# One more pair of K tiles through seven products in a feed-forward output projection

## The chip, the cores and the metric

The kernel runs on one NeuronCore of a Trainium2 chip. The metric is the device time of one execution in microseconds; the kernel before has a median of 1604.06 us over three runs. A change of some 0.2% of that, 3.2 us, is about what a measurement can tell from none.

## What is computed

The reference is one layer of an encoder over two sequences of 512 tokens with a model width of 1024: three branches (a state-space scan, a differential attention, a cross attention to a memory), their gated merge, and a gated feed-forward part with a hidden width of 2816. Only its last lines are touched here:

```
x = x + merged @ p['w_out'][l]
xn2 = _rmsnorm(x, p['norm_ffn'][l])
gate, up = jnp.split(xn2 @ p['w_ffn_in'][l], 2, axis=-1)
return x + (jax.nn.silu(gate) * up) @ p['w_ffn_out'][l]
```

After that comes a last `_rmsnorm` over the model width. All of it is float32. The product by `w_ffn_out` has 2816 = 22 x 128 rows to sum over, 22 **K tiles**, 8 output tiles of 128 model columns, and 1024 tokens (two sequences of 512).

## The kernel before, in words

**Precision by three matmuls.** Every operand is split into a rounded high part and the remainder (`split`, line 131: a cast on ACT at line 134 or 137 and a subtraction on DVE at line 135 or 138), and a product is three matmuls: high by high, high by low, low by high. One matmul has 128 rows of weights and up to 512 columns; all of them are issued at line 66. A matmul's result lies in one of eight PSUM banks, six under the tag `mm` and two under `tr` (line 928); a bank can be written anew when its reader is through.

**Seven products in place of eight.** A block of two by two tiles (two output tiles m and m+4, two K tiles 2p and 2p+1, the two sequences) can be multiplied with seven products of sums of tiles in place of eight, so 21 matmuls and not 24. Such a pair of K tiles needs, on the side of the activations, three sums on DVE and one on POOL (`quad_sums`, line 966), seven operands split into high and low (`quad_split`, line 983: four casts, four subtractions), and rooms for them (`quad_room`, line 977: four rooms in all, so pair i takes the room of pair i-4, and of i-4 only after its last matmul). A pair is made by `act_pair` (line 1117: two loads from DRAM, where the gated stage left its result `aD`, and the sums) and `pair_in` (line 1183). On the side of the weights it needs, for each of the four pairs of output tiles, a **piece**: seven sums of weight tiles with their splits. There are `NPAIR` x 4 pieces, and `NPREP` (line 40) says how each is got. The first 16 are wholly made beforehand, beside the attention, and written to DRAM; the next ones, up to the second number, have four of their seven made beforehand, in the gated stage (`prepare`, line 459, one half-piece per iteration by `half_piece`, line 491), and the other three made on the spot; the rest are wholly made on the spot (`weights7`, line 1213, with four additions on POOL in `raw_sums`, line 451).

**The gated stage.** The 22 tiles of the hidden width are made in a loop, each by seven products of four K blocks, 84 matmuls; the half-pieces are prepared in iterations 1 and on. Its pools are closed and the next stage's opened three iterations before the end.

**The visits.** The output projection goes in twelve visits (`VISITS`, line 35: a row m of output tiles and a range of pairs). A visit runs through its pairs, seven products each, adding up in seven banks; then seven sums on DVE (`quadrants`, line 1104, written at 1101) put the products together into four tiles, and four additions on POOL (line 1274) add them to the output y. For visit v the loop at line 1246 names where pairs are made: pair 4 within visit 3, others after visits 0, 1, 3, 4, 6 and 7. Weights for piece n+2 are loaded and for n+1 split while piece n is multiplied; their rooms rotate through six slots (`w_room`, line 1207).

**The plain part.** The K tiles that no pair takes (`nb` = 4 with nine pairs) are done by three matmuls each, at the end: first for the first sequence at 512 columns, then for each half of the second at 256. For every output tile DVE adds the bank to y (line 1345), ACT squares it, POOL adds the squares up (`sum_sq`, line 175). Then a root, a reciprocal and a transpose on PE (`factor`, line 195) give the norm, and eight scalings (line 1327 on DVE, some on POOL at line 1322) and the stores to the output follow (`final`, line 1313). The weights of the plain part are loaded in the last two visits (`keep`, line 1193) into rooms of a pair that has been used up, and split when the plain part begins; its four activations are split after visit 8 (line 1285 on).

**What sets the order.** From the last iteration of the gated stage to the end of the visits PE keeps the order in which the program is written; in the plain part and on the other engines a scheduler puts instructions in the order in which, by its own estimate, they can start, and in the order of the program where several can. Each engine then works through its list strictly in order. All transfers are issued from SP.

Of the kernel before, what the change touches and what calls it, by code (L numbers as in the profile page):

```python
# [19 lines left out]
P = 128  # L20
L = 512
# [7 lines left out]
KFF = FF // P  # L29
# [2 lines left out]
G = 32  # L32


VISITS = ((0, 0, 2), (1, 0, 3), (2, 0, 3), (3, 0, 4), (0, 2, 5), (1, 3, 6), (2, 3, 6), (3, 4, 7), (0, 5, 9), (1, 6, 9),
          (2, 6, 9), (3, 7, 9))
NPAIR = 9


NPREP = (16, 28)  # L40

NG = (7, 6, 3)

# [29 lines left out]
def encoder(ctx: ExitStack, tc: tile.TileContext, a, out):  # L73
    nc = tc.nc
# [31 lines left out]
    def slot(tag, shape=(P, NT), dt=F32, name="sl"):  # L106
        return pools[tag].tile(list(shape), dt, tag=tag, name=name)

    def bank(tag="mm"):
        return pools[tag].tile([P, 512], F32, tag=tag, name="bk" + tag)  # L110

    def aux():
        return bank("tr")
# [17 lines left out]
    def split(hi, lo, src, scale=None):  # L131

        if scale is None:
            h = S.copy(hi, src)  # L134
            l_ = V.tensor_tensor(out=lo, in0=src, in1=hi.bitcast(F32), op=ALU.subtract)  # L135
        else:
            h = S.activation(out=hi, in_=src, func=AF.Copy, scale=scale)
            l_ = V.scalar_tensor_tensor(out=lo, in0=src, scalar=scale, in1=hi.bitcast(F32), op0=ALU.mult, op1=ALU.subtract)
        return h, l_
# [47 lines left out]
    def rstd(acc, n, nt=4):  # L187


        ss = aux()  # L190
        for t in range(nt):
            PE.matmul(ss[:, t : t + 1], acc[:, t * P : (t + 1) * P], onec[:, 0:1], start=(t == 0), stop=(t == nt - 1))
        return factor(ss, n, nt)

    def factor(ss, n, nt=4, bias=epsc):

        rs = rp.tile([P, 4], F32, tag="rs", name="rs", bufs=4)
        S.activation(out=rs[:, :nt], in_=ss[:, :nt], func=AF.Sqrt, scale=1.0 / n, bias=bias)
        V.reciprocal(rs[:, :nt], rs[:, :nt])
        bc = aux()  # L200
        for t in range(nt):
            PE.transpose(bc[:, t * P : (t + 1) * P], rs[:, t : t + 1].broadcast_to([P, P]), ident)
        return rs, bc
# [89 lines left out]
    def queued():  # L293

        return tc.issue_after(last_w.ins)
# [54 lines left out]
    with yielding(last_s):  # L350
        x_norm(0, norm[0], range(5, 8))
        _, bc = factor(ss1, DM)
# [78 lines left out]
    for nm in ("c", "s"):  # L431
        r_ = rpp.tile([P, L], F32, tag=f"r{nm}", name=f"r{nm}")
# [4 lines left out]

    pieces = [(m, p) for m, lo_, hi_ in VISITS for p in range(lo_, hi_)]
    pieces = [(m, p, 7 if i < NPREP[0] else 4 if i < NPREP[1] else 0) for i, (m, p) in enumerate(pieces)]
    wD = {(m, p): drp.tile([P, n, 2, P], F32, name=f"wD{m}_{p}") for m, p, n in pieces if n}  # L440
# [18 lines left out]
    def prepare(es_, todo_):  # L459
        pq = es_.enter_context(tc.tile_pool(name="pq", bufs=1, side="right", reuse_waits="tile"))  # L460
        raws = []

        def load():
            if len(raws) < len(todo_):
                raws.append(pq.tile([P, 4, P], F32, tag="raw", name="raw", bufs=4))
                with queued():
                    raw_in(raws[-1], *todo_[len(raws) - 1][:2])

        def part(n_, j, w_):
            m, p, _ = todo_[n_]  # L470
            k = w_.shape[1]
            hl = pq.tile([P, k, 2, P], F32R, tag=f"hl{k}", name="hl", bufs=k // 2)
            split(hl[:, :, 0], hl[:, :, 1], w_, scale=0.5)
            nc.sync.dma_start(wD[m, p][:, j : j + k], hl.bitcast(F32))

        for _ in range(3):
            load()
        yield
        for n_, (m, p, k) in enumerate(todo_):
            load()  # L480
            if k == 7:
                part(n_, 4, raws[n_][:, 1:4])
            if k == 7 or n_ == 0:
                raw_sums(raws[n_])
                yield
            part(n_, 0, raws[n_])
            if n_ + 1 < len(todo_) and todo_[n_ + 1][2] == 4:
                raw_sums(raws[n_ + 1])
            yield
# [99 lines left out]
    pes = ExitStack()  # L589
    prep = prepare(pes, pieces[: NPREP[0]])  # L590
    next(prep)
# [87 lines left out]
    ld = lp.tile([P, 2], F32, tag="ld", name="ld", bufs=1)  # L679
# [11 lines left out]
    for i in range(-AHEAD, len(steps) + 1):  # L691
# [24 lines left out]
        if i > 0 and steps[i - 1][2] == 3:  # L716
            h, s, _ = steps[i - 1]
# [185 lines left out]
    n = len(steps)  # L903
# [73 lines left out]
    def quad_room(i):  # L977
        j = i // 2 % 2
        return slot(f"th{j}", [P, 7, L], F32R, "th"), slot(f"tl{j}", [P, 7, L], F32R, "tl")
# [3 lines left out]
    def quad_split(i, xa_, xb_, t_):  # L983

        nonlocal last_q
        th, tl = quad_room(i)
        split(th[:, 0], tl[:, 0], xa_[:, 0:L])
        split(th[:, 1:3].rearrange("p a n -> p (a n)"), tl[:, 1:3].rearrange("p a n -> p (a n)"), xb_)
        split(th[:, 3:5], tl[:, 3:5], t_[:, 0:2])
        last_q = split(th[:, 5:7], tl[:, 5:7], t_[:, 2:4])  # L990
        return th, tl
# [66 lines left out]
    aD = [drp.tile([P, NT], F32, name=f"aD{i}") for i in range(KFF)]  # L1058
# [75 lines left out]
    for i in range(KFF):  # L1134
        w = nxt_w or all7(i)
        nxt_w = None
        if i == 1:
            prep = prepare(pes, pieces[NPREP[0] : NPREP[1]])
            next(prep)
# [11 lines left out]
        if i == 0:  # L1151
            for s in range(NS):
                _, bc = rstd(accs[s], DM)
                S.copy(accs[s], bc)
        gf0, gf1, up0, up1 = quadrants(ps, p0)
        ac = ap2.tile([P, NT], F32, tag="ac", name="ac")
# [26 lines left out]
    def pair_in():  # L1183
        pairs.append(quad_split(len(pairs), *act_pair(len(pairs))))


    nb = KFF - 2 * NPAIR
    kept, lasts = [], []

    def last_rows(m):  # L1190
        return a["w_fo"][m, :, 2 * NPAIR * P :]

    def keep(n):
        if not kept:
            lasts.extend(quad_room(NPAIR + 1))
        for _ in range(n):
            i = len(kept)
            if i % 2 == 0:
                lasts[2:] = [slot("ld", [P, 2, L], name="fw")]
            k0, k1, raw = lasts  # L1200
            with queued():
                nc.sync.dma_start(raw[:, i % 2], last_rows(i + 1))
            kept.append((k0[:, i], k1[:, i], raw[:, i % 2]))

    n_w, last_7 = 0, None

# [38 lines left out]
    n_p = 0  # L1245
    for v, (m, lo_, hi_) in enumerate(VISITS):
        ps = [bank() for _ in range(6)] + [aux()]
        for p in range(lo_, hi_):
            if n_p + 2 < len(pieces):
                next(coming[n_p + 2])  # L1250
            for g in coming[n_p + 1 : n_p + 2]:
                for _ in g:
                    pass
            th, tl = pairs[p]
            w = made[n_p]
            n_p += 1
            if v < 4 and p == 1:
                with queued():
                    for t in (m, m + 4):
                        nc.sync.dma_start(y[t], x1D[t])  # L1260
            for p_, (nm, o) in zip(ps, SEVEN):
                wh, wl = w[nm]
                PE.matmul(p_, wh, th[:, o], start=(p == lo_), stop=False)
                PE.matmul(p_, wh, tl[:, o], start=False, stop=False)
                PE.matmul(p_, wl, th[:, o], start=False, stop=(p == hi_ - 1))
            if v == 3 and p == 0:
                pair_in()
            if (v, p) in ((10, 7), (10, 8), (11, 7), (11, 8)):
                keep(1 if v == 10 and p == 7 else 2)
        ps = iter(ps)  # L1270
        c11, c12, c21, c22 = quadrants(ps, next(ps), ("nsq", "nsq"))
        for c_, t, s in ((c11, 0, 0), (c22, 4, 1), (c21, 4, 0), (c12, 0, 1)):
            yv = y[m + t][:, s * L : (s + 1) * L]
            PO.tensor_tensor(out=yv, in0=yv, in1=c_, op=ALU.add)
        if v == 0:
            with tc.issue_after(last_sum.ins):
                pairs.append(quad_split(2, *nxt))
        elif v == 1:
            with queued(), tc.issue_after(last_sum.ins):
                pair_in()  # L1280
        for _ in range({3: 1, 4: 1, 6: 1, 7: 1}.get(v, 0)):
            pair_in()
        if v == 8:

            r0, r1 = quad_room(NPAIR)
            r2 = slot("ts", [P, 4, L], F32R, name="r2")
            room = [(r0[:, 2 * i : 2 * i + 2], r1[:, 2 * i : 2 * i + 2]) for i in range(3)] + [(r2[:, 0:2], r2[:, 2:4])]
            ah, al = [], []
            for i in range(2 * NPAIR, KFF):
                ac = slot("ld", name="fl")  # L1290
                nc.sync.dma_start(ac, aD[i])
                th, tl = (r_.rearrange("p a n -> p (a n)") for r_ in room[i - 2 * NPAIR])
                split(th, tl, ac, scale=0.5)
                ah.append(th)
                al.append(tl)
    PE.on = False


# [493 lines left out]
```

## Time and profile before

| | |
|---|---|
| median of three runs | 1604.06 us (1603.86 to 1604.61) |
| the profiled execution: span from first to last instruction | 1603.0 us |
| the profiled execution's own time | not listed apart from its span |
| mean granted clock of TensorE | 0.997 |
| PE busy | 1587.1 us, 99% |
| DVE busy | 1162.9 us, 73% |
| POOL busy | 541.6 us, 34% |
| bytes moved by the DMA queues | 237.86 MB, mean 148 GB/s |

In the profile PE is the matmul engine and PEld its loading of weights, DVE, ACT and POOL are the three others, SP issues the transfers. A row of the timeline is the start, the duration, the engine, the line, the operation, what it writes from what it reads, and in brackets how long its engine stood idle before it and what ended that. A busy time counts overlapping matmuls once. Times run from the span's start.

### The profile page before, as it was taken

Reading aid. Unit: us, or ns where it says so; the run is one execution under the profiler, and the core shown is the slowest. Engines: PE = TensorE matmul, PEld = TensorE weight load, DVE = VectorE, ACT = ScalarE, POOL = GpSimd, SP = SyncE. Lnnn points to the kernel's source line nnn. Section 1 sums busy time; section 2 is a strip of 40 time slices with the busy share of each in tenths; the row PEclk is TensorE's granted clock in tenths of the full one; section 3 lists DMA queues with packets and bytes.
Section 4 is the critical chain, followed back from the end, with each engine's and each line's share of the span. In section 5 each row is a group of like instructions: output and inputs, shape, how many; then the busy total and the mean of one; then the engine's idle time right before and its main releaser. Section 6 shows DMA issues by size and latency. Waiting matters only on the chain.

```text
span 1603.0 us, 21625 instructions
## 1 busy us (share of the span) xinstructions
PE 1587.1 (99%) x7838; PEld 1314.8 (82%) x7838; DVE 1162.9 (73%) x1856; ACT 640.0 (40%) x1142; POOL 541.6 (34%) x449
## 2 busy tenths in 40 slices
PE   9999999999999999999999999999999999999997
PEld 7888788888898778778878878888888888788877
DVE  7976996076773766776465678888898778988654
ACT  6544323274652455574133443332333323233323
POOL 0010100001333220300343367676665553444653
PEclk9999999999999999999999999999999999999998
DMA  9554523576762111244454432333323223986222
GB/s 366 173 160 150 179 95 125 180 273 201 252 224 102 54 47 40 73 156 140 145 190 132 144 118 80 131 119 129 121 106 118 79 88 119 344 332 198 80 66 106
DMA packets 104891, 237.86 MB, mean 148 GB/s; under 512 B 13520, under 2 KB 45008, under 8 KB 104784
## 3 DMA queue, kind: packets, MB, share of 16 engines
q1 hardware_dynamic: 104784, 236.47, 43.1%
q8 instruction: 62, 1.02, 0.3%
q14 instruction: 45, 0.37, 0.1%
HBM read 165.16 MB, written 71.27 MB: 147 GB/s over the span
## 4 chain that ended last, share of the span: by engine, by line
PE 87%; issue 4%; DVE 3%; DMA 3%; POOL 2%; ACT 0%; SPq 0%; POOLq 0%; DVEq 0%; ACTq 0%
PE bkmm L66 75%; PE bksc L66 3%; PE bktr L66 2%; PE bkoo L66 2%; PE bktr L69 2%; DVE tl L135 1%; PE bktr L1626 1%; POOL mg L793 1%; PE bktr L1597 1%; DMA yt<-bD 1%; PE bktr L1686 0%; PE bktr L1687 0%; PE bktr L1685 0%; PE bktr L1565 0%; DMA acc<-in_w_fo 0%
## 5 line engine op out<-in xcount | busy, mean ns | idle before, releaser
L66 PE MATMUL bkmm<-xh,wh 128*128 128x512 f32 x640 | 255.4, 399 | 0.0
L66 PE MATMUL bkmm<-xh,wl 128*128 128x512 f32 x640 | 250.9, 392 | 0.0
L66 PE MATMUL bkmm<-xl,wh 128*128 128x512 f32 x640 | 250.5, 391 | 0.0
L66 PE MATMUL bkmm<-tl,wh 128*128 128x512 f32 (+1 forms) x621 | 241.2, 388 | 1.4 <-DVE tl L135 1.4
L66 PE MATMUL bkmm<-th,wl 128*128 128x512 f32 (+1 forms) x621 | 241.0, 389 | 0.9 <-DVE wl L135 0.9
L66 PE MATMUL bkmm<-th,wh 128*128 128x512 f32 (+1 forms) x621 | 241.1, 389 | 0.0
L134 ACT CAST wh<-wf 128x1024 fp32r<-128x1024 f32 (+1 forms) x134 | 117.9, 880 | 224.1 <-PE bkmm L66 179.8
L135 DVE TENSOR_TENSOR wl<-wf,wh 128x1024 fp32r<-128x1024 f32 (+1 forms) x134 | 145.1, 1083 | 50.2 <-ACT wh L134 45.7
L66 PEld LDWEIGHTS bkmm<-xh,wh 128*128 128x128 f32 x640 | 120.3, 188 | 30.3 <-issue 7.9
L66 PE MATMUL bkmm<-th,w 128*128 128x512 f32 x432 | 141.5, 392 | 2.7 <-DVE up L1101 1.0
L66 PEld LDWEIGHTS bkmm<-xh,wl 128*128 128x128 f32 x640 | 120.2, 188 | 26.7 <-issue 1.3
L66 PEld LDWEIGHTS bkmm<-xl,wh 128*128 128x128 f32 x640 | 120.4, 188 | 22.4 <-issue 0.4
L66 PEld LDWEIGHTS bkmm<-tl,wh 128*128 128x128 f32 x621 | 116.6, 188 | 25.9 <-DVE tl L135 2.1
L66 PEld LDWEIGHTS bkmm<-th,wl 128*128 128x128 f32 x621 | 116.5, 188 | 25.7 <-DVE wl L135 1.7
L66 PEld LDWEIGHTS bkmm<-th,wh 128*128 128x128 f32 x621 | 116.6, 188 | 23.9
L1165 POOL TENSOR_TENSOR up<-up,acc 128x512 f32<-128x512 f32 x44 | 83.6, 1920 | 87.8 <-DVE up L1101 87.8
L454 POOL TENSOR_TENSOR raw<-raw 128x128 f32<-128x128 f32 x28 | 15.2, 545 | 284.4 <-DVE nb L545 206.5
L66 PEld LDWEIGHTS bkmm<-th,w 128*128 128x128 f32 x432 | 80.9, 188 | 23.8 <-DVE up L1101 3.4
L793 POOL TENSOR_TENSOR mg<-mg,gl 128x1024 f32<-128x1024 f32 x16 | 43.5, 2720 | 139.0 <-DVE gl L789 139.0
L548 ACT ACTIVATE e<-bksc,nb 128x512 f32<-128x512 f32 (+1 forms) x96 | 58.8, 615 | 73.5 <-DVE nb L543 51.9
L66 PE MATMUL bkmm<-tl,w 128*128 128x512 f32 x216 | 84.2, 390 | 0.0
L66 PE MATMUL bkmm<-yh,wh 128*128 128x512 f32 x192 | 75.9, 397 | 0.8 <-ACT wh L134 0.4
(641 smaller groups left out, 3527.8 us busy)
## 6 DMA issues: line engine op xcount, KB each, us to landing
wf<-in_w_in SPq DMA_DIRECT2D x40, 512.0 KB, 3.9
wD<-hl SPq DMA_DIRECT2D x28, 512.0 KB, 2.9
w<-wD SPq DMA_DIRECT2D x28, 512.0 KB, 5.0
gD<-gt SPq DMA_DIRECT2D x24, 512.0 KB, 2.8
gl<-gD SPq DMA_DIRECT2D x24, 512.0 KB, 3.4
wf<-in_w_fg SPq DMA_DIRECT2D x22, 512.0 KB, 3.7
wf<-in_w_fu SPq DMA_DIRECT2D x22, 512.0 KB, 3.6
aD<-ac SPq DMA_DIRECT2D x22, 512.0 KB, 3.1
```

The costliest lines, as they stand in the source:

```text
L66: return self.put(self.eng.matmul(*args, **kw))
L69: return self.put(self.eng.transpose(*args, **kw))
L134: h = S.copy(hi, src)
L135: l_ = V.tensor_tensor(out=lo, in0=src, in1=hi.bitcast(F32), op=ALU.subtract)
L454: PO.tensor_tensor(out=a22, in0=a21, in1=a22, op=ALU.add)
L548: last_x = S.activation(out=e, in_=sc, func=AF.Exp, bias=nb, scale=scale, accum_out=sm)
L793: PO.tensor_tensor(out=mg[m], in0=mg[m], in1=gt, op=ALU.add)
L1165: PO.tensor_tensor(out=up, in0=up, in1=accs[s], op=ALU.mult)
L1597: PE.matmul(kp[64 * hf : 64 * hf + 48, g * 144 : (g + 1) * 144], l_[:, 2 * hf + g, :], o_[:, 4 * g4 + 2 * hf + g, :], start=(l_ is lr48), ...
L1626: PE.matmul(ps[:, g * P : (g + 1) * P], w_[:, gg * P : (gg + 1) * P], u_[:, 8 * o + gg, :], start=True, stop=True)
```

## The change

Nine pairs become ten, and the plain part keeps two K tiles of 22 in place of four. Four pieces are added, one in each of visits 4, 9, 10 and 11 (with the new ranges of the visits), and the number that have four of seven weights made beforehand goes from 12 to 16, so that eight are still made on the spot. Pair 5 is now written within visit 3 and pairs 8 and 9 within visit 7. Weights kept for the plain part are 256 columns wide in place of 512 and lie side by side in one room; the two activations that are left are split after visits 9 and 10.

```
-VISITS = ((0, 0, 2), (1, 0, 3), (2, 0, 3), (3, 0, 4), (0, 2, 5), (1, 3, 6), (2, 3, 6), (3, 4, 7), (0, 5, 9), (1, 6, 9),
-          (2, 6, 9), (3, 7, 9))
-NPAIR = 9
-NPREP = (16, 28)
+VISITS = ((0, 0, 2), (1, 0, 3), (2, 0, 3), (3, 0, 4), (0, 2, 6), (1, 3, 6), (2, 3, 6), (3, 4, 7), (0, 6, 10), (1, 6, 10),
+          (2, 6, 10), (3, 7, 10))
+NPAIR = 10
+NPREP = (16, 32)
...
     def keep(n):
         if not kept:
-            lasts.extend(quad_room(NPAIR + 1))
+            lasts.extend(quad_room(NPAIR))
         for _ in range(n):
             i = len(kept)
             if i % 2 == 0:
-                lasts[2:] = [slot("ld", [P, 2, L], name="fw")]
-            k0, k1, raw = lasts
+                lasts[2:] = [slot("ld", [P, 2, nb * P], name="fw")]
+            raw = lasts[2][:, i % 2]
             with queued():
-                nc.sync.dma_start(raw[:, i % 2], last_rows(i + 1))
-            kept.append((k0[:, i], k1[:, i], raw[:, i % 2]))
+                nc.sync.dma_start(raw, last_rows(i + 1))
+            k0, k1 = (r_.rearrange("p a n -> p (a n)")[:, i * nb * P : (i + 1) * nb * P] for r_ in lasts[:2])
+            kept.append((k0, k1, raw))
+
+    ah, al = [], []
+
+    def last_act(i, th, tl):
+        ac = slot("ld", name="fl")
+        nc.sync.dma_start(ac, aD[i])
+        th, tl = (r_.rearrange("p a n -> p (a n)") for r_ in (th, tl))
+        split(th, tl, ac, scale=0.5)
+        ah.append(th)
+        al.append(tl)
...
-            if v == 3 and p == 0:
+            if (v, p) in ((3, 0), (3, 1), (7, 4), (7, 5)):
                 pair_in()
...
-        for _ in range({3: 1, 4: 1, 6: 1, 7: 1}.get(v, 0)):
+        elif v in (4, 6):
             pair_in()
-        if v == 8:
-
-            r0, r1 = quad_room(NPAIR)
+        elif v == 9:
             r2 = slot("ts", [P, 4, L], F32R, name="r2")
-            room = [(r0[:, 2 * i : 2 * i + 2], r1[:, 2 * i : 2 * i + 2]) for i in range(3)] + [(r2[:, 0:2], r2[:, 2:4])]
-            ah, al = [], []
-            for i in range(2 * NPAIR, KFF):
-                ac = slot("ld", name="fl")
-                nc.sync.dma_start(ac, aD[i])
-                th, tl = (r_.rearrange("p a n -> p (a n)") for r_ in room[i - 2 * NPAIR])
-                split(th, tl, ac, scale=0.5)
-                ah.append(th)
-                al.append(tl)
+            last_act(2 * NPAIR, r2[:, 0:2], r2[:, 2:4])
+        elif v == 10:
+            last_act(2 * NPAIR + 1, *(r_[:, 4:6] for r_ in lasts[:2]))
```

## The prediction

> **What bounds the kernel now.** I read the spans first, then the chain of work that ended last, then the table of stages (output of the gated part, its end, the visits, the plain part's first half, the rest), and last the timelines of PE, DVE, POOL and SP from 1460 us on.
>
> ```profile
> core 0: 1603.0 us, clock 0.997
> PE 87%; issue 4%; DVE 3%; DMA 3%; POOL 2%; ACT 0%; SPq 0%; POOLq 0%; DVEq 0%; ACTq 0%
> 975.00:1165.00 190.00, 190.00 (x839) 157.07 (x838) 168.48 (x183) 58.82 (x80) 127.48 (x95) 1.00 0.35 117
> 1165.00:1340.00 175.00, 175.00 (x774) 144.96 (x773) 141.86 (x161) 53.02 (x67) 96.34 (x56) 1.00 0.29 101
> 1367.00:1543.00 176.00, 173.33 (x752) 140.10 (x751) 142.01 (x174) 55.91 (x82) 89.92 (x84) 1.00 0.64 229
> 1543.00:1567.00 24.00, 23.07 (x103) 18.76 (x103) 11.73 (x19) 4.84 (x8) 12.70 (x10) 1.00 0.00 1
> 1567.00:1603.00 36.00, 27.82 (x228) 27.28 (x226) 17.37 (x39) 12.40 (x30) 12.30 (x18) 0.87 0.32 118
> ```
>
> The chain is 87% PE. PE is busy for the whole of the gated stage (190 of 190 us, 175 of 175) and idle for 2.7 us in the visits, so a matmul less there is time less, as long as DVE keeps up: it works 142 of 176 us in the visits. The stage table's columns are the stretch, its length and the busy time of PE, PEld, DVE, ACT and POOL. The clock is 1.00 wherever PE works. A recorded matmul (0.39 us) overlaps the next, so I price by distances between starts:
>
> ```profile
> 1474.51 0.39 PE L66 MATMUL bktr<-th,w 128*128 128x512 f32 x1
> 1479.27 0.39 PE L66 MATMUL bktr<-th,w 128*128 128x512 f32 x1
> 1549.76 0.61 PE L66 MATMUL bkmm<-r,th 128*128 128x512 f32 x2
> 1552.47 0.61 PE L66 MATMUL bkmm<-r,th 128*128 128x512 f32 x2
> 1569.27 0.40 PE L66 MATMUL bkmm<-r,th 128*128 128x256 f32 x2
> 1570.71 0.40 PE L66 MATMUL bkmm<-r,th 128*128 128x256 f32 x2
> ```
>
> The first two rows are the ends of two neighbouring pieces (one pair of K tiles for one pair of output rows, 21 matmuls): 4.76 us a piece. The next two are one output tile of the plain part apart, 4 K tiles with 3 matmuls each: 2.71 us at 512 columns, 0.226 a matmul. The last two are the same at 256 columns: 1.44 us, 0.120 a matmul, more than half of 0.226.
>
> **Step 1, PE's work.** The plain part has 8 tiles at 512 and 16 at 256: 8 x 2.71 + 16 x 1.44 = 44.7 us. With 2 K tiles instead of 4 half of it goes: **-22.35 us**. Pair 9 adds four pieces, one in each of visits 4, 9, 10 and 11: 4 x 4.76 = **+19.04**. Net **-3.3 us**. All of it lies on the path. (The Trainium skill, TensorE: Matmul & The Clock Gate, section Back-to-back issue gap, gives 262 cycles for 256 columns and 518 for 512, a ratio of 0.506; the trace disagrees, 1.44/2.71 is 0.53. By the page the 256-column part would give back 0.55 us less and the net would be an estimated -2.8.)
>
> **Step 2, the first plain weight.**
>
> ```profile
> 1539.83 4.78 DVE L135 TENSOR_TENSOR tl<-fw,th 128x512 fp32r<-128x512 f32 x6
> 1544.54 0.68 DVE L135 TENSOR_TENSOR wl<-wf,wh 128x512 fp32r<-128x512 f32 x1
> 1545.75 0.68 DVE L1101 TENSOR_TENSOR u<-bkmm,p 128x512 f32<-128x512 f32 x1
> 1545.27 0.50 PE L66 MATMUL bkmm<-th,wl 128*128 128x512 f32 x1 [0.93 <-DVE wl L135]
> ```
>
> The plain part starts 0.93 us late (1.05 with the refill), since the low half of its first weight waits behind six splits of kept weights. After, each is 256 columns wide; the nearest row of DVE at that width is five additions in 1.74 us (step 4), 0.35 each. The six take about 2.1 instead of 4.78 and the stall goes: **-1.05**. Against it: by the rotation of weight rooms the slot of that load now comes free one piece, 4.76 us, before it is needed, and the load of it with its two casts must fit there. Bounds: -1.05 to +1. I take the first, because the transfer is half as large.
>
> **Step 3, the visits.** DVE does not follow the program's order: by the rows below pair 5, written after visit 3, is split by 1424.3, before that visit's first sum (1424.97), and pair 8, written after visit 7, by 1480.96, before 1481.35. So placing them inside the visits moves little. What is new is pair 9 in visit 7, beside pair 8:
>
> ```profile
> 1419.63 0.68 DVE L135 TENSOR_TENSOR tl<-fa,th 128x512 fp32r<-128x512 f32 x1
> 1421.97 2.35 DVE L135 TENSOR_TENSOR tl<-ts,th 128x1024 fp32r<-128x1024 f32 x2
> 1424.97 0.68 DVE L1101 TENSOR_TENSOR u<-bkmm,p 128x512 f32<-128x512 f32 x1
> 1429.30 0.50 PE L66 MATMUL bkmm<-th,w 128*128 128x512 f32 x1 [0.36 <-DVE up L1101]
> 1461.72 1.76 SPq L1291 DMA_DIRECT2D fl<-aD  x2
> 1465.48 1.54 POOL L972 TENSOR_TENSOR ts<-fb,fa 128x512 f32<-128x512 f32 x1 [5.83 <-DVE tl L135]
> 1465.79 1.78 DVE L971 TENSOR_TENSOR ts<-fa 128x512 f32<-128x512 f32 x1
> 1477.47 1.21 DVE L135 TENSOR_TENSOR tl<-fb,th 128x1024 fp32r<-128x1024 f32 x1
> 1478.61 2.35 DVE L135 TENSOR_TENSOR tl<-ts,th 128x1024 fp32r<-128x1024 f32 x2
> 1481.35 0.68 DVE L1101 TENSOR_TENSOR u<-bkmm,p 128x512 f32<-128x512 f32 x1
> 1484.03 0.39 PE L66 MATMUL bktr<-th,w 128*128 128x512 f32 x1
> L138 DVE SCALAR_TENSOR_TENSOR w<-acc,w 128x384 fp32r<-128x384 f32 (+1 forms) x28 | 25.0, 896 | 23.4 <-ACT w L137 23.4
> 1490.70 4.30 DVE L138 SCALAR_TENSOR_TENSOR tl<-fl,th 128x1024 fp32r<-128x1024 f32 x3 [0.20 <-ACT th L137]
> ```
>
> Visit 7's seven sums begin at 1481.35; the visit ends on PE at 1484.03 + 0.23 = 1484.26. Pair 9 has its loads early (two slots of that pool were free at 1461.7), but its sums need the single room of pair 8's, free only at 1480.96. Its work on DVE is three sums of 0.68 (the width of the split at 1419.63) and splits of 0.68, 1.21 and 2.35: 6.3 us. Room in the whole: from 1480.96 to the fourth piece of visit 8 (1484.26 + 3 x 4.76 = 1498.5) are 17.6 us for 6.3, the seven sums (7 x 0.68 = 4.8) and four weight splits (0.9 each, 3.6): 14.7. It fits, as the splits of the last activations (4.30 for three) leave this place. So the cost is one of order. Visit 8's second product needs its bank at 1484.94 and the first sum is through at 1482.03: 2.9 us may stand ahead of the sums for nothing. If half of pair 9's 6.3 us and one weight split of 0.9 come ahead, 4.1 us do: **+1.2**. Bounds: 0 (sums first) and 5.5 (all of it first, 8.4 at the slow durations below, less 2.9).
>
> By the row at 1465.79 an addition takes 1.78 us instead of 0.68 while POOL runs one. That is what the Trainium skill's SBUF — State Buffer, section Who interferes with whom, states: a DVE instruction with two SBUF inputs contends with a GpSimd one that reads SBUF, and the later waits. Nothing in the sum hangs on the page; by it pair 9 takes an estimated 8.4 us when two such meetings fall in it, not 6.3.
>
> The other edits cost nothing that I can find. Four pieces more are prepared in the gated stage, in iterations 14 to 17:
>
> ```profile
> 1135.68 3.91 POOL L1165 TENSOR_TENSOR up<-up,acc 128x512 f32<-128x512 f32 x2 [0.47 <-DVE up L1101]
> 1154.49 3.91 POOL L1165 TENSOR_TENSOR up<-up,acc 128x512 f32<-128x512 f32 x2 [0.48 <-DVE up L1101]
> 1267.41 3.90 POOL L1165 TENSOR_TENSOR up<-up,acc 128x512 f32<-128x512 f32 x2 [6.01 <-DVE up L1101]
> 1286.45 3.90 POOL L1165 TENSOR_TENSOR up<-up,acc 128x512 f32<-128x512 f32 x2 [6.02 <-DVE up L1101]
> ```
>
> An iteration with such a piece turns round in 18.81 us on DVE and POOL, one without in 19.04, which is PE's 84 matmuls. PE hides it with 0.23 us to spare; without that cover, each of the four would cost some tenths. Eight pieces are still made on the spot, as before, at the same last places, so their part of the 2.7 us of idle PE stays. The transfers of the four (0.5 MB written, 0.7 MB read each) fall where the DMA share is 0.29 and 0.64.
>
> **Step 4, the end.** This is where the saving is at risk. The plain part is done per sequence: sums, norm, scaling, output, with the next columns' matmuls beside it.
>
> ```profile
> 1565.79 1.28 POOL L182 TENSOR_TENSOR acc<-acc,nsq 128x512 f32<-128x512 f32 x1 [1.44 <-ACT nsq L181]
> 1566.53 0.39 PE L66 MATMUL bkmm<-r,tl 128*128 128x512 f32 x1
> 1576.19 5.36 DVE L1327 SCALAR_TENSOR_TENSOR y<-y,vec,bktr 128x512 f32<-128x512 f32 x8 [0.73 <-PE bktr L69]
> 1581.46 1.74 DVE L1345 TENSOR_TENSOR y<-y,bkmm 128x256 f32<-128x256 f32 x5
> 1591.87 0.87 DVE L1327 SCALAR_TENSOR_TENSOR y<-y,vec,bktr 128x256 f32<-128x256 f32 x2 [1.16 <-ACT acc L1319]
> 1592.45 0.36 PE L66 MATMUL bkmm<-r,tl 128*128 128x256 f32 x1
> ```
>
> The first half's matmuls end at 1566.76; its eight scalings on DVE end at 1581.55, **14.8 us later**. PE meanwhile works on the two quarters and ends them at 1592.6, 25.9 us after 1566.76, of which 16 x 1.44 = 23.0 are matmuls: the block is covered with 11 us over. After, the quarters take 11.5 + 2.9 = 14.4 us, and the lag does not shrink: POOL needs 1.28 us a tile for the sums of squares, a tile now comes every 1.36, and POOL enters late, with the last visit's four additions before it. So the scalings end when the last matmul could. The additions of the second quarter (0.35 each) wait behind them in DVE's queue, PE has six banks and stops when they are full, and two of the next four scalings (0.43) stand there too: six to eight additions and 0.87 are 3.0 to 3.6 us, of which 0.6 would be there anyway. I take **+3.0**. Bounds: 0, if the scheduler puts the additions first, and 6.2, the whole block of 5.36 with 0.87 behind it. From the last addition to the last output, some 10 us, nothing changes.
>
> **Sum:** -3.3 - 1.05 + 1.2 + 3.0 = -0.15 us. The profiled execution spans 1603.0, 1.0 below the median 1604.06; the difference is put on the median: **1603.9 us**. PE's gain is eaten by the shorter cover at the end.
>
> **Rivals.**
> - The end stays PE's (chance 0.21). For it: six free banks let additions slip ahead of the scalings, and the seven sums of the last visit, begun at 1545.75 before, move forward with step 2. Against it: the five additions at 1581.46 stand right behind the scalings. Then steps 3 and 4 cost nothing: 1604.06 - 4.35 = 1599.7.
> - Pair 9 wholly ahead of visit 7's sums (0.17). It is written ahead of them now, its room is free 0.4 us before the first sum, and POOL's additions of visit 6 run then. DVE's queue would hold 8.4 us where 2.9 are free; it decides from the point where more than half of the pair comes first. The price is 5.5 in place of 1.2: 1608.2, slower. Against it: after visit 3, with pair 5 right ahead of the sums, the longest wait of PE was 0.36 us.
> - The scalings exposed in full (0.10): 6.2 in place of 3.0 gives 1607.1.
> - The forecast (0.52), with 1601.5 to 1606.3 as its own range.
>
> A measurement can tell about 0.2%, 3.2 us, from no change. **Faster** is the first rival, 0.21. **Slower** is the second, and the third where a little of step 3 joins it: 0.19. The rest, 0.60, is **within**. The range reaches almost to the first rival and up to the second: 1600.0 to 1608.2.
>
> **What would show it.** Right: the plain part's PE rows at 1.36 and 0.72 us a tile; its first matmul without a wait; PE waiting on DVE's additions to the output (line 1345 before) in the last quarter; the block of eight scalings ending near the last matmul. Wrong: no idle time there (step 4 too dear), a wait of over 2 us at the start of visit 8 on DVE sums (step 3 too cheap), or any PE wait in the gated stage.

## The result, and the profile after

The changed kernel takes **1610.2 us** (median of five runs, 1609.84 to 1610.98) against 1604.06 before; the ratio is 1.0040, with a 95% interval of 1.0029 to 1.0051. It is slower, by 6.1 us, where 1603.9 was forecast, and lies above the forecast's range of 1600.0 to 1608.2. The profiled execution took 1610.98 us with a span of 1609.2; the span before was 1603.0, so the spans differ by 6.2, and the accounts below are made on them.

The span of the changed kernel with its clock:

```profile
core 0: 1609.2 us, clock 0.994
```

The table of stages of the changed kernel (stretch, length, busy time of PE, PEld, DVE, ACT, POOL with their counts, clock, DMA share, GB/s), the last three stretches moved to where the stages lie now:

```profile
975.00:1165.00 190.00, 190.00 (x839) 157.13 (x838) 168.53 (x182) 58.92 (x80) 129.12 (x95) 1.00 0.35 117
1165.00:1340.00 175.00, 175.00 (x774) 144.96 (x773) 149.62 (x165) 54.64 (x71) 108.39 (x73) 1.00 0.35 118
1367.00:1562.00 195.00, 188.36 (x814) 152.89 (x813) 146.58 (x180) 54.90 (x78) 92.51 (x83) 0.99 0.62 217
...
1574.00:1609.00 35.00, 23.52 (x158) 21.88 (x156) 19.78 (x43) 15.38 (x36) 20.46 (x24) 0.80 0.33 121
```

In the gated stage PE is as full as before (190 of 190, 175 of 175), though DVE and POOL do more there. In the visits it is not: PE is idle for 6.6 us of 195 where it was idle for 2.7 of 176. And after 1574 it is idle for 11.5 of 35 us.

Where the visits lose shows in the timeline of PE at the start of visit 8 (start, duration, engine, line, operation; in brackets PE's idle time and what ended it):

```profile
1491.50 0.50 PE L66 MATMUL bkmm<-th,w 128*128 128x512 f32 x1 [1.00 <-DVE u L1101]
...
1494.85 0.50 PE L66 MATMUL bkmm<-th,w 128*128 128x512 f32 x1 [1.71 <-DVE u L1101]
...
1497.18 0.50 PE L66 MATMUL bkmm<-th,w 128*128 128x512 f32 x1 [1.37 <-DVE up L1101]
...
1498.91 0.60 PE L66 MATMUL bkmm<-th,w 128*128 128x512 f32 x1 [0.77 <-DVE nsq L1101]
...
1502.30 0.76 PE L66 MATMUL bkmm<-th,w 128*128 128x512 f32 x2
```

Four times PE waits for a bank that one of visit 7's sums (line 1101) has to empty: 4.85 us by the brackets, 5.5 by the distances between starts, less the usual 0.226. (A bracket begins only where the record of the matmul before it ends, 0.16 us after the next could have started.) Then eight matmuls, from 1498.91 to 1502.30, stand 0.43 us apart and not 0.226: 1.6 us more. Stretches of 2 us, in the columns of the table of stages, show the clock that goes with it:

```profile
1490.00:1492.00 2.00, 1.00 (x5) 0.54 (x4) 2.00 (x5) 1.05 (x1) 0.00 (x0) 1.00 0.56 162
...
1496.00:1498.00 2.00, 0.82 (x3) 0.49 (x3) 2.00 (x3) 0.00 (x0) 0.79 (x1) 1.00 0.05 15
1498.00:1500.00 2.00, 1.23 (x4) 0.88 (x4) 2.00 (x4) 1.06 (x1) 2.00 (x2) 0.79 0.00 0
1500.00:1502.00 2.00, 2.00 (x6) 1.52 (x6) 2.00 (x2) 0.52 (x1) 2.00 (x2) 0.50 0.03 8
1502.00:1504.00 2.00, 2.00 (x9) 1.65 (x8) 1.26 (x1) 0.00 (x0) 0.84 (x1) 0.86 0.00 0
```

Where the mean falls to 0.79, 0.50 and 0.86 the clock was halved for 0.84 + 2 + 0.56 = 3.4 us. Together that is 7.1 us. The first matmul after each wait is slow too (0.34 us from 1491.50 to the next start), and so is the last pair at the halved clock, so that visit 8's start loses some 7.5 us in all. The timeline of DVE in the changed kernel says why the sums are late:

```profile
1486.26 0.54 DVE L138 SCALAR_TENSOR_TENSOR w<-acc,w 128x384 fp32r<-128x384 f32 x1
1486.73 1.78 DVE L971 TENSOR_TENSOR ts<-fa 128x512 f32<-128x512 f32 x1
1488.43 0.68 DVE L135 TENSOR_TENSOR tl<-fa,th 128x512 fp32r<-128x512 f32 x1
1489.03 1.21 DVE L135 TENSOR_TENSOR tl<-fb,th 128x1024 fp32r<-128x1024 f32 x1
1490.17 0.68 DVE L973 TENSOR_TENSOR ts<-fb,ts 128x512 f32<-128x512 f32 x1
1490.77 0.68 DVE L1101 TENSOR_TENSOR u<-bkmm,p 128x512 f32<-128x512 f32 x1
...
1491.97 0.67 DVE L974 TENSOR_TENSOR ts<-fb,ts 128x512 f32<-128x512 f32 x1
1492.57 1.63 DVE L138 SCALAR_TENSOR_TENSOR w<-acc,w 128x384 fp32r<-128x384 f32 x1
1494.12 0.68 DVE L1101 TENSOR_TENSOR u<-bkmm,u 128x512 f32<-128x512 f32 x1
...
1495.32 1.21 DVE L135 TENSOR_TENSOR tl<-ts,th 128x1024 fp32r<-128x1024 f32 x1
1496.45 0.68 DVE L1101 TENSOR_TENSOR up<-bkmm,u 128x512 f32<-128x512 f32 x1
1497.05 1.21 DVE L135 TENSOR_TENSOR tl<-ts,th 128x1024 fp32r<-128x1024 f32 x1
```

Lines 971, 973, 974 and 135 are pair 9: two of its sums and two of its splits stand ahead of the first of visit 7's sums, the rest lies between the seven. DVE is never idle here; it works in an order that holds PE up.

The plain part starts at the first row below in the kernel before, at the second in the changed one:

```profile
1543.73 0.39 PE L66 MATMUL bkmm<-th,wh 128*128 128x512 f32 x1
```
```profile
1568.66 0.62 PE L66 MATMUL bkmm<-r,wh 128*128 128x512 f32 x2
```

It starts 24.9 us later, of which 19.04 are the four new pieces. Another 0.8 has nothing to do with the visits: their first matmul starts at 1367.33 where it started at 1366.50 before, and a row of POOL ahead of the gated stage (line 793) already at 836.99 instead of 836.12. Why is open; among the profiled executions of all runs that first matmul lies anywhere from 1366.42 to 1369.16. So the visits cost 5.1 more (visit 8's 7.5 less small waits that are gone, as those of 0.31 at 1528.64 and 0.30 at 1539.96 before). From there to the end of the span it takes 40.5 us instead of 59.3. The end of the changed kernel, first PE, then DVE:

```profile
1592.68 0.28 PE L66 MATMUL bkmm<-th,tl 128*128 128x256 f32 x1
1597.10 0.69 PE L69 MATMUL bktr<-ident,rs 128*128 128x128 f32 x2 [4.14 <-DVE rs L199]
...
1598.30 2.70 PE L66 MATMUL bktr<-onec,nsq 128*128 128x1 f32 x12
```
```profile
1590.96 5.35 DVE L1330 SCALAR_TENSOR_TENSOR y<-y,vec,bktr 128x512 f32<-128x512 f32 x8
1596.22 0.75 DVE L1348 TENSOR_TENSOR y<-y,bkmm 128x256 f32<-128x256 f32 x2
1596.89 0.16 DVE L199 RECIPROCAL rs<-rs 128x2 f32<-128x2 f32 x1
1596.96 0.40 DVE L1348 TENSOR_TENSOR y<-y,bkmm 128x256 f32<-128x256 f32 x1
```

The last matmul of the plain part starts at 1592.68, without a wait before it. Then PE waits 4.14 us for the third quarter's reciprocal (the norm of the first half of the second sequence), which stands in DVE's queue behind the eight scalings of the first sequence. The last three additions to the output stand there too.

### The profile page after: what moved, and what is told of

The parts are those of the page before. It is cut to its first block, busy times and chain, and to the rows that moved or that the text cites. A ratio compares the mean times of both kernels' runs of the same rounds, so it can differ in the third digit from the quotient of the medians.

```text
span 1609.2 us, 21586 instructions
## 1 busy us (share of the span) xinstructions
PE 1584.9 (98%) x7778; PEld 1311.7 (82%) x7778; DVE 1173.3 (73%) x1869; ACT 643.6 (40%) x1152; POOL 558.8 (35%) x466
## 4 chain that ended last, share of the span: by engine, by line
PE 92%; DVE 4%; issue 1%; POOL 1%; DMA 1%; ACT 1%; SPq 0%; POOLq 0%; DVEq 0%; ACTq 0%
PE bkmm L66 79%; PE bktr L66 3%; PE bksc L66 3%; PE bkoo L66 2%; PE bktr L69 2%; DVE tl L135 2%; PE bktr L1629 1%; POOL acc L182 1%; PE bktr L1600 1%; PE bktr L1690 0%; PE bktr L1689 0%; PE bktr L1688 0%; PE bktr L1568 0%; DMA mt<-in_memT 0%; DMA fa<-aD 0%
## 5 line engine op out<-in xcount | busy, mean ns | idle before, releaser
L66 PE MATMUL bkmm<-tl,wh 128*128 128x512 f32 x615 | 239.3, 389 | 1.4 <-DVE tl L135 1.4
L66 PE MATMUL bkmm<-th,wh 128*128 128x512 f32 x615 | 239.2, 389 | 0.0
L66 PE MATMUL bkmm<-th,wl 128*128 128x512 f32 x615 | 238.9, 389 | 0.0
L66 PE MATMUL bkmm<-th,w 128*128 128x512 f32 x480 | 157.5, 393 | 6.6 <-DVE u L1101 2.9
L66 PEld LDWEIGHTS bkmm<-th,w 128*128 128x128 f32 x480 | 90.7, 189 | 29.4 <-DVE u L1101 4.1
L66 PE MATMUL bkmm<-tl,w 128*128 128x512 f32 x240 | 94.0, 392 | 0.0
```

The costliest lines, as they stand in the source:

```text
L66: return self.put(self.eng.matmul(*args, **kw))
```

## The experiments

About the visits the theory is **order**, that pair 9's work costs since the scheduler puts it ahead of visit 7's sums and between them; its rivals are the place of pair 9 in the program and the amount of work on DVE. About the end: that the **block of scalings** in front of the third quarter's reciprocal is the loss, against the chain of the norm itself.

**Sums first.** Pair 9 is made behind visit 7's last sum.

```
-            if (v, p) in ((3, 0), (3, 1), (7, 4), (7, 5)):
+            if (v, p) in ((3, 0), (3, 1), (7, 4)):
...
+        elif v == 7:
+            with tc.issue_after(last_sum.ins):
+                pair_in()
```

> Pair 9's additions and splits on DVE are forced behind the last of visit 7's seven sums; nothing else changes. Theory A (the time is lost at the start of visit 8, where the sums stand behind pair 9: waits of PE of 1.15 + 1.86 + 1.53 + 0.93 = 5.5 us, and eight matmuls at 0.43 instead of 0.23 us, 1.6 us): nearly all of the 7.1 us comes back, less up to 1 us where visit 8's fourth piece may wait for pair 9: 1603 to 1604.5 us, and no half-rate matmuls. Theory B (DVE has too much work there in any order): the wait moves to the fourth piece of visit 8, and the time stays above 1608. Theory C (the loss is at the end of the plain part): 1610 unchanged.

Measured: 1603.04 (11 runs, 1601.98 to 1603.91), ratio to before 0.9990 (0.9981 to 0.9998): 7.2 us off the changed kernel. DVE of this run:

```profile
1487.14 0.69 DVE L1101 TENSOR_TENSOR u<-bkmm,p 128x512 f32<-128x512 f32 x1 [0.36 <-ACT p L1107]
...
1491.93 0.68 DVE L1101 TENSOR_TENSOR nsq<-bktr,p 128x512 f32<-128x512 f32 x1
1492.53 1.17 DVE L971 TENSOR_TENSOR ts<-fa 128x512 f32<-128x512 f32 x1
...
1498.26 2.36 DVE L135 TENSOR_TENSOR tl<-ts,th 128x1024 fp32r<-128x1024 f32 x2
```

The seven sums run from 1487.14 to 1492.6, with one weight split among them, pair 9 is ready at 1500.6, and PE neither waits at the start of visit 8 nor slows down. The end is as it was (40.6 us from the start of the plain part): the gain lies in the visits alone.

**The place in the program.** Pair 9 written after visit 7, with nothing that forces an order.

```
-            if (v, p) in ((3, 0), (3, 1), (7, 4), (7, 5)):
+            if (v, p) in ((3, 0), (3, 1), (7, 4)):
...
-        elif v in (4, 6):
+        elif v in (4, 6, 7):
             pair_in()
```

> Pair 9 is written after visit 7, as pair 8 was in the kernel before, without any forced order. Theory A with the order made by the scheduler and not by the place in the program: DVE's order is the same but for one split, so the wait at visit 8 stays and the time is 1609 to 1611 us. If the place in the program were the cause: about 1604 us.

Measured: 1610.48 (five runs), ratio 1.0037 (1.0024 to 1.0050). DVE's order is that of the changed kernel but for one split. PE's first three waits are the same (1.02, 1.70 and 1.37 us) and half rate follows, here from the third wait on and for longer:

```profile
1497.07 0.79 PE L66 MATMUL bkmm<-th,w 128*128 128x512 f32 x1 [1.37 <-DVE up L1101]
```

The fourth wait is gone, as PE at half rate comes to that bank later. The place in the program is not the cause: the scheduler's own order is.

**No work for pair 9.** Its products read pair 8's operands; its loads, sums and splits are left out.

```
+        elif v == 7:
+            pairs.append(pairs[8])
```

> Leaves out the loads, sums and splits of pair 9: the matmuls of pair 9 read pair 8's operands again, so the matmuls are all there and DVE's 6.3 to 8.4 us of pair 9 are not. Theory A: the whole wait at visit 8 goes, with the half-rate matmuls: 1602.5 to 1603.5 us, the same as with the sums first within 1 us. Theory B: clearly less (by 2 us or more) than with the sums first. Theory C: 1610.

Measured: 1602.66 (ten runs, 1602.00 to 1603.94), ratio 0.9992 (0.9983 to 1.0001). That is the time of the sums-first version within its spread, so pair 9's work on DVE costs nothing measurable once it stands behind the sums.

**One scaling left** (built on sums first; seven of the first sequence's eight scalings are left out).

```
+                    if c0 or m < 1:
                         V.scalar_tensor_tensor(out=y[m][:, cs], in0=y[m][:, cs], scalar=vcol("norm_final", m), in1=bc[:, :n],
```

> Built on e1_sums_first; leaves out seven of the eight scalings of the first sequence, so that part of the output stays unscaled. It takes the whole block (5.35 us) but one of 0.67 from DVE. If the block alone makes the wait of 4.14 us for the reciprocal: the wait falls to some tenths and the median to 1598.6 to 1599.3. If the wait is the chain of the norm itself (square, sum, root, reciprocal), it stays over 2 us and the median is above 1601.

Measured: 1598.25 (four runs), a little under the 1598.6 to 1599.3 expected; ratio 0.9963 (0.9949 to 0.9977). PE of this run:

```profile
1584.42 0.40 PE L69 MATMUL bktr<-ident,rs 128*128 128x128 f32 x2 [0.21 <-DVE rs L199]
1585.36 0.61 PE L66 MATMUL bktr<-onec,acc 128*128 128x1 f32 x4 [0.53 <-POOL acc L182]
```

The wait of 4.14 is 0.21, and the stretch from the plain part's first matmul to the end falls from 40.6 to 36.3 us. The block is the loss at the end. The run takes 4.7 us of work off DVE altogether, so it does not tell whether another order could win the loss back; the next four runs try that.

**Half the scalings late.** Four scalings of the first sequence come behind the last addition (on the changed kernel itself).

```
+            with tc.issue_after(last_add.ins):
+                for _ in end0:
+                    pass
...
-        if c != L:
+        if c == 0:
+            end0 = end
+            for _ in range(4):
+                next(end0)
+        if c > L:
             for _ in end:
```

> Of the first sequence's eight scalings the last four are written behind the last addition of the plain part, so DVE has 2.7 us less ahead of the reciprocal on which PE waits 4.1 us near the end. If the tail is dear because that block stands in DVE's queue: 1610.2 - 2.7 + at most 0.5 = 1607.5 to 1608.0 us. If the end is set by POOL's sums of squares or by the outputs instead: 1610 or more.

Measured: 1611.45 (five runs), ratio 1.0045 (1.0032 to 1.0058): a miss. PE of this run:

```profile
1593.89 0.43 PE L69 MATMUL bktr<-ident,rs 128*128 128x128 f32 x2 [1.51 <-DVE rs L199]
...
1596.93 0.83 PE L66 MATMUL bktr<-onec,acc 128*128 128x1 f32 x4 [2.61 <-DVE y L1330]
```

The wait for the reciprocal falls from 4.14 to 1.51 as it should, and a wait of 2.61 takes its place: the last norm's sums need one of the two `tr` banks, and the delayed scalings still read it.

**Sums first, half the scalings late, another bank for the last norm's sums.** The two edits above, and:

```
-                ss = aux()
+                ss = bank()
```

> Built on e1_sums_first (median 1603.04, PE waits 4.14 us for the reciprocal of the third quarter behind eight scalings of the first sequence). Four of the eight scalings are let go only behind the last addition, and the last column sums go into a bank of the six instead of one of the two that the scalings hold. If the block of scalings in front of that reciprocal is what step 4 lost, and the bank of the column sums is what ate the gain in e3_half_scalings_late: 4 x 0.67 = 2.7 us come off the wait of 4.14, none of it returns as a wait for the scalings, and the median is 1600.4 to 1601.0. If it is PE's or ACT's part of the norm that ends last, the wait moves and the median stays at 1603.0 +- 0.5.

Measured: 1603.47 (11 runs, 1602.57 to 1604.63), ratio 0.9992 (0.9983 to 1.0001): no gain over 1603.04, a second miss. With a bank at hand the scheduler put the last norm's column sums ahead of the last two tiles' matmuls, where PE waits 2.67 us for POOL, and the last reciprocal stands behind eight scalings of 4.29 us.

**Late behind the last reciprocal.** The four scalings go behind the last reciprocal, the sums over the first tiles come last, and the last factor takes a bank of the six too.

```
+            next(end)
+            with tc.issue_after(last_rs.ins):
+                for _ in end0:
+                    pass
             for _ in end:
...
-            ones(ss, sq, n, stop=(m == KD - 1))
+            ones(ss, sq, n, start=(m == KD - 3))
+            if m == KD - 1:
+                ones(ss, acc, n, stop=True)
```

> Built on e1_sums_first (1603.04; one scaling left in e8: 1598.25). Four of the eight scalings of the first sequence are let go only behind the last reciprocal; the last norm's sums and its factor take banks of the six, and its sums over the first five tiles come last in PE's order, so that PE doesn't wait for POOL in front of two tiles of matmuls as in e4_sums_first_half_late (2.67 us). If e4 failed only since two new waits (that one, and the last reciprocal behind eight scalings of 4.29 us) ate its gain: the third quarter's reciprocal comes 2.7 us earlier, the last one some 4, then nine scalings (2.7 + 2.05) end the work on DVE, and the median is 1600.0 to 1601.0. If DVE's total work after the last matmul is what bounds the end, moving it cannot help: 1603.0 +- 0.5.

Measured: 1604.54 (11 runs, 1602.85 to 1606.59), ratio 0.9998 (0.9989 to 1.0007). A third miss. PE of this run:

```profile
1585.94 0.43 PE L69 MATMUL bktr<-ident,rs 128*128 128x128 f32 x2 [2.71 <-DVE rs L202]
1586.37 1.01 PE L66 MATMUL bkmm<-onec,nsq 128*128 128x1 f32 x4
```

The transposes of the third quarter's norm now stand ahead of the last two tiles on PE, so PE waits 2.71 us with matmuls still to do, and those follow at half rate, 1.28 us a tile.

**The last tiles ahead of the norm.** As the last, with PE's order put right.

```
-                    for _ in range((0, 0, 1, 2, 3)[m]):
-                        next(end)
...
         if c > L:
-            for _ in end:
-                pass
+            with tc.issue_after(last_mm.ins):
+                for _ in end:
+                    pass
```

> As e6_late_behind_last_reciprocal (1604.54), but PE gets the last two tiles' matmuls ahead of the third quarter's transposes and of the last norm's column sums, as e1_sums_first had them. In e6 PE waited 2.71 us for the third quarter's reciprocal in front of those tiles, and the matmuls behind that wait ran at half rate (1.28 us a tile for 0.72). If that wait and the half rate ate what the halved block gave: the last tile ends near 1585, the last reciprocal comes near 1588.5 instead of 1593.4, nine scalings (4.75 us) and the store follow, and the median is 1599.0 to 1600.5. If the block of scalings was no loss that can be got back by order alone, the median stays at 1603 to 1604.

Measured: 1602.29 (11 runs, 1600.97 to 1603.88), ratio 0.9988 (0.9979 to 0.9997): of all complete versions the fastest, 0.12% under the kernel before, less than what a measurement can tell from none. It is above the 1599.0 to 1600.5 that were expected, and within the spread of sums first. DVE of this run:

```profile
1589.31 1.66 DVE L1336 SCALAR_TENSOR_TENSOR y<-y,vec,bktr 128x256 f32<-128x256 f32 x4 [2.63 <-ACT acc L1328]
1590.88 0.16 DVE L202 RECIPROCAL rs<-rs 128x2 f32<-128x2 f32 x1
1590.95 2.71 DVE L1336 SCALAR_TENSOR_TENSOR y<-y,vec,bktr 128x512 f32<-128x512 f32 x4
```

The last reciprocal comes at 1590.88 instead of 1593.69 (sums first), 2.8 us earlier, and the four delayed scalings take 2.71 of it again. DVE stood idle for 2.63 us ahead of that; what of it a better order could still fill wasn't tried.

**What halves the clock** (three runs built on the version without pair 9's work; the half rate above goes with a halved clock). Extra DVE operations hold up visit 7's sums: twelve or six ahead of the first, or two ahead of each of the seven.

```
+                V.tensor_tensor(out=t_, in0=t_, in1=t_, op=ALU.max)
```

> Built on e7_no_pair9_work (median 1602.66, no wait at visit 8, no work for pair 9). Twelve additional DVE operations of 0.6 us on one operand (in place, values unchanged) stand ahead of the first sum of visit 7 and delay it, with two weight splits, to about 1496; PE should wait once, some 5.5 us, at the second product of visit 8, and the later banks come free faster than PE needs them. If the half rate of the matmuls in the changed kernel comes from the long stretch with little PE work, whether chopped or in one piece: a stretch at 0.43 us a matmul follows here too, and the median is 1602.7 + 5.5 + 1.6 = 1609.8. If it takes work chopped by waits: no half rate, 1608.2.

Measured: 1612.32 (four runs), ratio 1.0046 (1.0032 to 1.0060). PE of this run:

```profile
1497.15 0.79 PE L66 MATMUL bkmm<-th,w 128*128 128x512 f32 x1 [7.08 <-DVE u L1101]
1497.74 0.63 PE L66 MATMUL bkmm<-tl,w 128*128 128x512 f32 x1
```

One wait of 7.08 us, not the 5.5 expected, and half rate behind it: the work need not be chopped by several waits.

> Built on e7_no_pair9_work. Two additional DVE operations of 0.6 us ahead of each of visit 7's seven sums: by the order of the banks PE should wait three times about 2.2 us with 1.4 us of work between, 6.6 in all, with no single wait over 2.5. If chopped waits bring the half rate as in the changed kernel: some eight matmuls at 0.43 us, +1.6, and a median of 1602.7 + 6.6 + 1.6 = 1610.9. If it takes one wait of over 3.4 us: no half rate, 1609.3.

Measured: 1615.0 (four runs), ratio 1.0065 (1.0051 to 1.0079). PE of this run:

```profile
1493.19 0.50 PE L66 MATMUL bkmm<-th,w 128*128 128x512 f32 x1 [2.28 <-DVE gf L1101]
...
1498.11 0.50 PE L66 MATMUL bkmm<-th,w 128*128 128x512 f32 x1 [3.26 <-DVE up L1101]
...
1502.39 0.79 PE L66 MATMUL bkmm<-th,w 128*128 128x512 f32 x1 [3.31 <-DVE nsq L1101]
```

The waits are longer than aimed at (2.28, 3.26, 3.31), so this run doesn't separate short waits from long ones; half rate (0.79 for a recorded matmul) again follows.

> As d1_one_long_wait (median 1612.32: one wait of 7.08 us, after it matmuls at 0.43 us until 1501.5), with six additional operations in place of twelve: one wait of about 3.5 us. In d1 the granted clock fell some 4.5 us after PE stopped. If the clock needs that long with no or little work, it doesn't fall here and the cost is the wait: 1602.7 + 3.5 = 1606.2. If it falls after every wait longer than 3 us: some 1.6 us more, 1607.8.

Measured: 1607.26 (ten runs, 1605.37 to 1609.72), ratio 1.0017 (1.0008 to 1.0026). PE of this run, and its clock in stretches of 2 us:

```profile
1494.50 0.50 PE L66 MATMUL bkmm<-th,w 128*128 128x512 f32 x1 [2.69 <-DVE u L1101]
...
1496.48 0.63 PE L66 MATMUL bkmm<-tl,w 128*128 128x512 f32 x1
```
```profile
1496.00:1498.00 2.00, 2.00 (x6) 1.56 (x5) 2.00 (x4) 0.00 (x0) 1.50 (x2) 0.50 0.00 0
1498.00:1500.00 2.00, 2.00 (x7) 1.58 (x7) 0.03 (x1) 0.16 (x1) 2.00 (x3) 0.67 0.03 8
```

The run does not answer its question as it was put: the wait is 2.69 us, not 3.5, and the clock halves behind it all the same. The ten times fall in two groups, four from 1605.37 to 1606.12 and six from 1607.11 on. The wait, 2.85 us by the distance between starts, on 1602.66 gives 1605.5; the half-rate stretch of the profiled execution (1609.36, one of the six) adds some 1.8. That the clock held in the four fits this, and fits their mean granted clock (0.995 to 0.996 against 0.994 to 0.995; 3.4 us at half clock make 0.001). It is not shown, since only one was profiled, and that one was already 2.5 us late ahead of the gated stage (a row of POOL's line 793 at 838.80, in the version without pair 9's work at 836.34).

## Why the prediction was wrong, step by step

**Step 1, PE's work: right.** Nothing measured speaks against 4.76 us a piece or -22.35 for the plain part, whose tiles come at 1.36 and 0.72 us; the sum below closes with them.

**Step 2, the first plain weight: right.** The row at 1568.66 has no wait; the 1.05 us are gone, and the six splits of 256 columns take 2.09 us where 2.1 was forecast. (By the distances between starts the loss before was 1.2.)

**The pieces in the gated stage: right.** They cost nothing; PE is busy for 190 of 190 and 175 of 175 us.

**Step 3, the visits: the step that failed.** It put +1.2 on the guess that half of pair 9 and one weight split come ahead of visit 7's sums. What came ahead of the first sum was pair 9's 1.78 + 0.68 + 1.21 + 0.68, less overlaps 4.0 us (1486.73 to 1490.77), and one weight split of 0.54. That much is near the 4.1 assumed, and the first wait is 1.15 us by the starts, near the forecast. The failure is in what follows: pair 9 did not end there, and another 0.67, 1.63 (a weight split beside POOL's addition), 1.21 and 1.21 came in between the seven sums, so that PE waited four times, 5.5 us in place of 1.2. And the clock was no part of the working: 1.6 more. ("The clock is 1.00 wherever PE works" holds for the busy stretches of its table; the last row of the same table has 0.87.) With the slow first matmuls visit 8's start loses 7.5, and since some 2.4 of other waits went, the stage came to +5.1.

The rival that put pair 9 wholly ahead of the sums had the right cause, and its price of 5.5 is what the waits come to; it gave 1608.2, without the clock. That its number fits is partly luck, as pair 9 lay half ahead of the sums and half among them. The argument against it, that pair 5 stood ahead of the sums of visit 3 at a wait of 0.36, weighed more than what the rival itself had noted, that pair 9's room comes free just ahead of the sums. So it was: pair 8's last splits end at 1486.3, pair 9's first sum starts at 1486.73, and visit 7's sums could have started at 1487.14, as they do in sums first.

**Step 4, the end: mechanism right in part, size too small.** It took +3.0 and measured +4.6: 40.5 us where 59.3 - 22.35 - 1.05 = 35.9 would be without it. It had the block of eight scalings (5.35 us here) come to stand in front of the last additions, and so it does: with one scaling left 36.3 remain, 0.4 above 35.9. Three things were off.

First, the block does not end with the last matmul but 3.5 us behind it (1596.3 and 1592.8): it ends 16.8 us behind the first sequence's matmuls (1579.54 to 1596.31), not 14.8 as before, and the two quarters take 13.3 us, not 14.4. Second, PE never ran out of banks; no row of it in the plain part has a wait before that of 4.14 us for the third quarter's reciprocal. Third, the stretch from the last addition to the last output, which it had called unchanged, grew from 9.7 to 11.8 us. The last addition before:

```profile
1592.85 0.42 DVE L1345 TENSOR_TENSOR y<-y,bkmm 128x256 f32<-128x256 f32 x1
```

It ended 0.8 us behind the start of the last plain matmul (1592.45); in the changed kernel it is 4.7 (1592.68 to 1597.36), and behind it the last norm finds the third quarter's transposes ahead of its own sums on PE, at a clock of 0.50. Together the stretch from that matmul's start to the end is 16.5 us, 10.5 before. Up to that matmul the plain part took 1.3 us less than 48.7 - 22.35 - 1.05, hence 4.6 and not 6.

The sum: -3.3 - 1.05 + 5.1 + 4.6, and 0.8 from ahead of the gated stage, make +6.15; measured by the spans, 6.2. Of the 6.3 us by which the forecast of -0.15 was off, step 3 has 3.9, step 4 1.6 and the unexplained offset 0.8.

Of the rivals, the one in which the end stays PE's falls with the wait of 4.14 us. The 4.6 of the end lies midway between the forecast's 3.0 and the 6.2 of the rival with the scalings exposed in full.

## What to carry to other kernels

When two pieces of preparation share a room, the second starts when the first ends, and a scheduler that goes by its own estimates may deal it out between the operations that empty the next stage's banks. So count everything that is ready at that moment, not a half of it, and force the bank-emptying operations ahead: a few lines were worth 7.2 us here. Saving matmuls where a block on another engine is just covered gives back little until that block moves, and moving half of it behind the critical chain gave almost nothing, since it only came back there (the last reciprocal 2.8 us earlier, 2.71 spent behind it, the median 0.75 lower).

## What the runs showed of the hardware that was not expected

**A wait of PE can cost more than its length.** In the visits of the changed kernel no wait of PE is over 1.71 us, but it is busy for only 3.92 of the 8 us from 1490 to 1498 (1.00 in the first two, 0.82 in the last), and then the clock is halved for 3.4 us: 1.6 us on top of 5.5. One wait of 2.69 us did it too, in the profiled execution of that run, and so did waits of 2.67 and 2.71 us ahead of tiles still to do.

The profiles show a pattern that no run was built to test. The clock is halved for 3.4 us in the changed kernel (1499.16 to 1502.57) and with six extra operations (1495.92 to 1499.33), and for 6.8 us with pair 9 written after visit 7, with twelve extra operations and with two ahead of each sum. In the 3.4 us ahead of these five falls PE was busy for 1.27, 1.42, 1.36, 0.00 and 0.91 us. In the 3.4 us before those, at whose end the clock held, it was busy for 1.70, 2.71, 2.39, 2.34 and 1.66 us. So PE's work in such a stretch parts the two cases here, between 1.42 and 1.66 us, and the longest single wait does not: the 1.71 us lie in a stretch that kept the clock.

The Trainium skill, TensorE: Matmul & The Clock Gate, section HAM oscillation — how this bites in real kernels, gives the rule that idle gaps above some 3.4 us are what counts; the trace disagrees, as gaps of no more than 1.71 and 2.69 us were enough. The Trainium skill, TensorE: Matmul & The Clock Gate, section A second HAM failure mode: psum-queue depth-cycling, describes frequent short idling between groups of matmuls that makes the clock go up and down; that fits the changed kernel.

**Two inputs beside POOL.** The addition at 1486.73 took 1.78 us, that at 1490.17 0.68; line 138's split of 384 columns took 0.54 at 1486.26 and 1.63 at 1492.57. POOL adds at 1486.41 (1.54 us) and at 1492.12 (1.66 us), so each of these two meetings cost DVE some 1.1 us. The operations that paid had started while POOL's addition ran; the split at 1486.26 and the sum at 1491.97 (0.67 us), already running when POOL began, did not.
